# HGRN score matmuls in two stretches per head, the diagonal by products on GpSimd

## The chip, the cores and the metric

One core of one Trainium2 chip runs the whole program in one launch. The metric is the device time in microseconds (us) of one execution, and the comparison is the median over several executions. Engines are called PE (matrix engine), DVE (vector engine), ACT (scalar engine), POOL (GpSimd) and SP (the engine that issues most DMAs).

## What is computed

The reference is one inference step of a layer with two parallel branches, an mLSTM and an HGRN2, merged by sigmoid gates. A prompt of 512 frames and a running stream of 32 frames go through together (544 columns). The change touches only the HGRN2 branch: 8 heads of width 128, in which every head computes, in chunks of 64 frames,

```python
g = cumsum(lf)                                  # per channel, lf = log of the forget gate
dec = exp(where(causal, g[t] - g[s], -inf))
a = einsum('tc,tsc,sc->ts', q, dec, k)          # scores, decay per channel
o = einsum('tc,ce->te', q * exp(g), S) + einsum('ts,se->te', a, v)
S_new = exp(g_last)[:, None] * S + einsum('sc,se->ce', k * exp(g_last - g), v)
```

and then a head-wise RMS norm of `o`, times a gate. All is float32.

## The kernel before

**Layout.** Activations lie with channels on the 128 partitions and frames along the free dimension. The kernel treats the 512 prompt frames of a head as chunks of 128 (`chunks`), the first half in reversed order, with the 32 sample frames between the halves (`HB` = 288 is the border, `NA` = 256, `NS` = 32).

**Dense work.** PE runs the projections, those of the HGRN branch and the merge gates among them, as dense matmuls with 272 moving columns (`Two.run`, L609). Each weight is split into a high and a low part on ACT (L133) and DVE (L134), and some weight sums are formed by DMA: SP loads a tile (L495), POOL starts a second transfer that adds into it (L496), and a third one may follow (L582). POOL's DMA starts sit in the same in-order queue as its other instructions.

**The pump.** PE's order in this part is written by hand. `Pump.run` takes a generator and, for each number it yields, advances the dense stream by so many steps; one step is six dense matmuls. The generator is `chain(h)`, one per HGRN head; its matmuls are placed between the dense ones where it resumes. The instructions of the other engines are ordered by the scheduler, by priority; `tc.high_priority()` lifts what stands under it. A chain takes 28 steps (27 for head 0), as many as the dense work of one head, so that one chain follows the other.

**A chain.** The causal decay is applied level by level (`LEVELS` = 1, 2, 4, 8, 16, 32, 64). At level c, blocks of c keys meet the next block of c queries; then keys and queries are multiplied in place by the decay over c frames, on DVE (L1911, two halves, with the decay products `tn` built at L1914 and L1917). For each level PE multiplies a packed copy of the keys (`km`, ACT, L1879) with the queries, for four groups of 32 keys side by side (L1841), plus four matmuls for the sample frames on levels under 32 (L1844). Because the products are made in place, levels 2, 8 and 32 also take a packed copy of the queries (`oldq`, L1873) and of the sample's pair (`olds`, L1878), so that two levels can be multiplied in one stretch of PE. This gives four stretches of score matmuls in a head: the diagonal with level 1, levels 2 and 4, 8 and 16, 32 and 64.

The diagonal (q times k of the same frame, summed over channels) is made by 20 matmuls of 32 keys against 32 queries (L1894), of which DVE keeps the diagonal by a product with a mask (`eye`, L1921) and a reduction (L1922) into `dg`. ACT scales the transposed values by it into `ov` and `osb` (L1946, L1947), and DVE adds that to the output later (L1996, L1997).

`collect` brings scores from PSUM into the tile `at` (L1854 on DVE under a level mask, L1856 and L1860 on ACT). POOL spreads `near` and `far` into place (L1935) and cuts the triangles into `aa` (L1790). The rest of the chain: transposes of the values (`columns`, L1818, right after level 1), of the keys, the state update `su` (L1966, DVE L1972), and the output `ho` (L1990 to L1994). Then ACT squares the output (L2001, L2002), DVE computes the inverse root and scales (L2006, L2012). `finish(h - 1)` transposes the output of the head before and multiplies by its gate. PSUM for all of these comes from `paux`, a ring of two buffers.

## Time and profile before

| | |
|---|---|
| median of 3 runs | 1091.46 us (1091.30 to 1091.87) |
| the profiled execution | 1093.22 us in all, span 1091.5 us |
| granted PE clock | 1.00 |
| PE busy | 1082.2 us (99%) |
| DVE busy | 896.1 us (82%) |
| ACT busy | 700.6 us (64%) |
| POOL busy | 220.1 us (20%) |
| DMA | 176.67 MB, mean 162 GB/s |

A row of a group of instructions names line, engine, operation, output and inputs with their shapes, then the count; behind the bar stand the busy time in us and the mean ns of one, and behind the next bar the idle time just ahead of them with what ended most of it. A row of the timeline starts with the start in us from the beginning of the span and the duration; a count at its end means that several like it were merged. A row by stretch gives the window, its length, and then the busy us of PE, its weight loads, DVE, ACT and POOL. A row of waits gives who waited for whom, the total, how often, and the longest. A float32 matmul appears as two records; the dense matmuls with rounded operands (L609) as one.

### The profile page before, as it was taken

The numbers are of one execution on the slowest core, as the hardware profiler recorded it, in microseconds if no ns is written. First come the engines' busy times: TensorE is split into PE (matmuls) and PEld (weight loads), VectorE is DVE, ScalarE is ACT, GpSimd is POOL, SyncE is SP. The second block draws the span as 40 slices with busy tenths as digits, with TensorE's granted clock in tenths as the row PEclk, the third lists the DMA queues.
The fourth block names the chain that finished last, engine by engine and source line by source line (L and its number), as shares of the span: only waits on it lengthen the run. The fifth ranks groups of instructions, "written<-read, shape, count | busy, mean of one in ns | idle before, by whom it ended". The sixth has DMA issues, their size and how long they took to land.

```text
span 1091.5 us, 26220 instructions
## 1 busy us (share of the span) xinstructions
PE 1082.2 (99%) x9865; PEld 1055.3 (97%) x9865; DVE 896.1 (82%) x2052; ACT 700.6 (64%) x1611; POOL 220.1 (20%) x399
## 2 busy tenths in 40 slices
PE   9999999999999999999999999999999999999998
PEld 9899999999999999999999999999999999999997
DVE  7889988686897785986888688989999877778886
ACT  7767556754666564765557378877777666446673
POOL 5204010303021122202120032323333210000002
PEclk9999999999999999999999999999999999999999
DMA  7134515549454377545699666666666683337753
GB/s 237 54 124 145 173 59 175 152 135 211 131 170 154 122 171 168 176 164 176 187 245 256 184 158 138 150 152 157 152 146 160 172 225 98 112 91 243 232 199 121
DMA packets 97270, 176.67 MB, mean 162 GB/s; under 512 B 11412, under 2 KB 18580, under 8 KB 96888
## 3 DMA queue, kind: packets, MB, share of 16 engines
q1 hardware_dynamic: 81072, 140.96, 40.5%
q0 software_dynamic: 15184, 32.93, 16.6%
q8 instruction: 77, 1.26, 0.5%
q10 hardware_dynamic: 888, 1.12, 0.3%
q14 instruction: 49, 0.40, 0.1%
HBM read 150.05 MB, written 41.69 MB: 176 GB/s over the span
## 4 chain that ended last, share of the span: by engine, by line
PE 89%; DVE 4%; DMA 4%; issue 1%; ACT 1%; POOL 0%; ACTq 0%; DVEq 0%; SPq 0%; POOLq 0%
PE d L609 41%; PE ya L168 9%; PE yb L168 4%; PE q L168 4%; PE k L168 4%; PE C L1078 4%; PE sc L1038 2%; PE u L292 2%; PE d L461 2%; PE vp L1570 2%; PE nm L1258 2%; DMA ws<-in_w_in 2%; PE ple L168 1%; PE pl L1841 1%; DMA kv_d<-vhl 1%
## 5 line engine op out<-in xcount | busy, mean ns | idle before, releaser
L496 POOL DMA_DIRECT2D ws<-in_w_in x46 | 40.2, 875 | 198.0 <-DVE hkq L1911 61.2
L623 ACT COPY t<-d 128x272 f32<-128x272 f32 x153 | 57.9, 378 | 15.6 <-PE d L609 14.6
L1911 DVE TENSOR_TENSOR hkq<-hkq,q 128x288 f32<-128x288 f32 (+1 forms) x96 | 40.6, 429 | 4.0 <-PE pl L1844 3.4
L786 DVE SCALAR_TENSOR_TENSOR cv<-ub,vec,cv 128x547 f32<-128x547 f32 x48 | 37.6, 783 | 1.7 <-ACT cv L781 1.2
L1192 DVE SCALAR_TENSOR_TENSOR c<-c,wi,Cs 128x258 f32<-128x258 f32 x32 | 15.3, 479 | 18.8 <-PE Cs L1190 18.5
L1355 DVE TENSOR_TENSOR y<-ya,y 128x272 f32<-128x272 f32 x48 | 18.8, 434 | 14.3 <-PE ya L168 12.5
L1090 ACT COPY Co<-C 128x258 f32<-128x258 f32 x30 | 9.8, 378 | 27.2 <-PE C L1078 24.9
L778 POOL COPY uo<-ub 128x3 f32<-128x3 f32 x16 | 18.7, 1166 | 34.6 <-DVE ub L632 26.7
L134 POOL TENSOR_TENSOR wple50l<-wple5r,wple50h 128x256 fp32r<-128x256 f32 x1 | 0.7, 736 | 121.1 <-ACT wple50h L133 121.1
L962 POOL COPY ksm<-kf 128x96 f32<-128x96 f32 x16 | 7.1, 445 | 85.8 <-ACT kf L976 85.7
L1269 ACT COPY y<-nm 128x516 f32<-128x516 f32 x16 | 9.4, 590 | 22.9 <-PE nm L1258 22.5
L1879 ACT COPY km<-hkq 128x256 f32<-128x256 f32 x56 | 23.7, 424 | 0.0
L1935 POOL COPY at<-at 32x128 f32<-32x128 f32 x32 | 21.7, 678 | 8.4 <-DVE wa1282l L134 6.7
L962 POOL COPY vsm<-vt 128x96 f32<-128x96 f32 x12 | 5.7, 478 | 86.4 <-ACT vt L634 44.1
L582 POOL DMA_DIRECT2D ws<-in_w_in x14 | 12.8, 915 | 38.6 <-DVE ws272l L134 27.6
L1246 DVE BATCH_NORM_STATS2 bs<-y 128x6 f32<-128x512 f32 (+1 forms) x20 | 13.8, 691 | 8.2 <-ACT y L1269 7.8
L1258 PE MATMUL nm<-vhl,sh 128*128 128x258 f32 x112 | 18.4, 286 | 0.0
L2001 ACT ACTIVATE osq<-kq 128x128 f32<-128x128 f32 x32 | 9.8, 305 | 13.4 <-DVE kq L1996 13.1
L377 POOL DMA_DIRECT2D w_pg_d<-in_w_pg x16 | 13.1, 818 | 24.4 <-issue 20.2
L377 POOL DMA_DIRECT2D w_out_d<-in_w_out x16 | 13.5, 1004 | 14.3 <-issue 12.5
L1790 POOL TENSOR_SCALAR_AFFINE_SELECT aa<-at 128x128 f32<-128x128 f32 x32 | 16.1, 536 | 0.6
L1258 PEld LDWEIGHTS nm<-vhl,sh 128*128 128x128 f32 x112 | 15.4, 190 | 0.5 <-ACT Co L1090 0.3
(4739 smaller groups left out, 5095.3 us busy)
## 6 DMA issues: line engine op xcount, KB each, us to landing
ws<-in_w_in POOLq DMA_DIRECT2D x60, 256.0 KB, 5.1
ws<-in_w_in SPq DMA_DIRECT2D x46, 256.0 KB, 4.3
ya_d<-y SPq DMA_DIRECT2D x32, 272.0 KB, 2.3
y<-ya_d SPq DMA_DIRECT2D x24, 272.0 KB, 3.6
w_out_d<-in_w_out POOLq DMA_DIRECT2D x24, 256.0 KB, 6.6
w_pg_d<-in_w_pg POOLq DMA_DIRECT2D x24, 256.0 KB, 6.5
c<-in_C SPq DMA_DIRECT2D x16, 258.0 KB, 3.7
out_Cs<-c SPq DMA_DIRECT2D x16, 258.0 KB, 4.0
```

The costliest lines, as they stand in the source:

```text
L168: PE.matmul(both[b][:m, :TH], part(w, off + k * step, m, x), xx[:, half(b)], start=(k == 0 and j == 0), stop=(k == n - 1 and j == 2),)
L292: PE.matmul(both[b][:m, :TH], part(w, off + k * step, m, x), xx[:, half(b)], start=(k == 0 and j == 0), stop=(k == KD - 1 and j == 2),)
L377: G.dma_start(late[g][n][k], src, accum_op=ALU.add)
L461: PE.matmul(self.ps[b][:, : c.stop - c.start], part(self.w, k * P, P, x), xx[:, c], start=(k == 0 and j == 0), stop=(k == KD - 1 and j == 2),)
L496: G.dma_start(t, piece(u, i), accum_op=ALU.add)
L609: PE.matmul(ps, ww[:, c], xx, start=(start and k == 0 and j == 0), stop=end, skip_group_check=not start,)
L623: self.kept = S.copy(t, ps)
L786: V.scalar_tensor_tensor(cv[:, :547], ub[:, j : j + 547], vcol(V_CW + 4 * ft + j), cv[:, :547], ALU.mult, ALU.add)
L1078: PE.matmul(pn[g][:, :VH], kw[b][x][:, f * P : (f + 1) * P], vv[b][y][:, g * VH : (g + 1) * VH], start=(b == 0 and j == 0), stop=(b == NB ...
L1258: PE.matmul(pn[:, g, :VH], st[j][x][:, (i - j) * P : (i - j + 1) * P], vv[j][y][:, g * VH : (g + 1) * VH], start=(j == 0 and q == 0), stop ...
L1879: low = S.copy(km.rearrange("p (n j c) -> p n j c", j=2, c=c), view(kk, HB, ((2 * c, NA // (2 * c)), (c - HB, 2), (1, c))),)
L1911: V.tensor_tensor(x, x, d, ALU.mult)
```

## The change

The scores of a head are computed in two stretches instead of four: the diagonal with levels 1, 2, 4 and 8, and then levels 16, 32 and 64. For that, levels 1, 2, 4, 16 and 32 take packed copies of the queries (and levels 1, 2, 4 and 16 of the sample's pair), in tiles whose buffers other phases used (`more`, `asked`, `far_`, and the tile `q0`); level 64 reads its keys in place without a copy. The decay products `tn` move from `q0` into `tf`.

The diagonal: POOL multiplies queries and keys element by element (`q0 * kk`), and 20 matmuls against a matrix of two columns of ones sum over the channels. DVE copies the result to `dg`. POOL multiplies the identity by it into `ov` and adds that into the triangles `aa` (and, for the sample, into `near`), so the output matmul includes the diagonal. The scalings on ACT and the additions on DVE go; the squares and the scaling read the output from PSUM.

The steps between the parts of the chain change (`STEPS`, `TAILS`; 28 in all again), and levels 1 and 2 lose their high priority (`URGENT`).

```diff
-STEPS = (2, 3, 3, 3, 3, 3, 3)
+STEPS = (2, 2, 2, 4, 2, 2, 3)
+BEHIND, URGENT, TAILS = (1, 3, 5, 6), 2, (3, 2, 4)
+FIRSTS, LASTS = (0, 4), (3, 6)
...
             V.tensor_tensor(qq[:, :T], q0[:, :T], tf[:, :T], ALU.mult)
+            G.tensor_tensor(q0[:, :T], q0[:, :T], kk[:, :T], ALU.mult)
...
         for li, c in enumerate(LEVELS):
-            first_ = li % 2 == 1
-            if li % 2 == 1 or li == 0:
+            if li in FIRSTS:
                 kms = tp.tile([P, 2, NA], F32, tag="vs", name=f"km{h}{c}", bufs=1)
-            km = kms[:, 0 if li % 2 else 1]
+                if li == 0:
+                    more, asked = (tp.tile([P, NA + 4 * NS], F32, tag=g, ...) ... (("kx", "ksm"), ("qx", "vsm")))
+                    far_ = tp.tile([P, 2, NA], F32, tag="kws", name=f"kqx{h}", bufs=1)
+                    keeps = [(kms[:, 0], old), (kms[:, 1], asked[:, :NA]), (more[:, :NA], far_[:, 0]), (far_[:, 1], None)]
+                    rest = [more[:, NA : NA + 2 * NS], more[:, NA + 2 * NS :], asked[:, NA : NA + 2 * NS]]
+                else:
+                    keeps = [(kms[:, 0], q0[:, :NA]), (kms[:, 1], q0[:, NA : 2 * NA]), (None, None)]
+                    rest = [more[:, NA : NA + 2 * NS]]
+                held_ = []
+            n, last = len(held_), li in LASTS
+            km, oldq = keeps[n]
...
-            with tc.high_priority():
-                if first_:
+            with tc.high_priority() if li >= URGENT else nullcontext():
+                if not last:
                     S.copy(oldq..., view(qq, ...))
                     if c < NS:
                         S.copy(olds, hs[h]["pair"][:, :, csmp])
-                low = S.copy(km..., view(kk, ...))
-            if not first_:
+                if km is not None:
+                    low = S.copy(km..., view(kk, ...))
+            if li in BEHIND:
                 held.append(low)
-                yield STEPS[li] + (STEPS[li - 1] if li else 0)
-                pn = paux(f"pl{h}{c}")
-                if li:
-                    scores(pn, 0, c // 2, kms[:, 0], True)
-                else:
-                    ...  PE.matmul(pn[...], kk[:, t_], q0[:, t_], start=True, stop=True)
-                scores(pn, 1, c, km, False)
+            yield STEPS[li]
+            if last:
+                pn, at_ = paux(f"pl{h}{c}")[:, 0], 0
+                if li == LASTS[0]:
+                    ...  PE.matmul(pn[..., 2 * b : 2 * b + 2], q0[:, t_ : t_ + NS], ones, start=True, stop=True)
+                    at_ = 4 * NS
+                outs_ = []
+                for li_, c_, km_, oldq_, olds_ in held_:
+                    w = 3 * NS if c_ < NS else 2 * c_
+                    outs_.append((pn[:, at_ : at_ + w], li_, c_))
+                    scores(outs_[-1][0], c_, km_, oldq_, olds_)
+                    at_ += w
...
-            if not first_:
-                if li == 0:
-                    same = small("same", [P, NB + 1, NS], bufs=1, tag="vsm")
-                    V.tensor_tensor(same, pn[...], eye, ALU.mult)
-                    V.tensor_reduce(dg, same, AX.X, ALU.add)
-                else:
-                    collect(pn[:, 0], li - 1, c // 2)
-                collect(pn[:, 1], li, c)
+            if last:
+                for x in outs_:
+                    collect(*x)
+                if li == LASTS[0]:
+                    V.tensor_copy(dg, pn[:, : 2 * (NB + 1) : 2])
+                    G.tensor_tensor(ov[:, :NP]..., ident..., dg[:, :NB]..., ALU.mult)
+                    G.tensor_scalar(ov[:, NP:T], ident[:, :NS], dg[:, NB : NB + 1], None, ALU.mult)
+                    G.tensor_tensor(near[:, 2 * NS :], near[:, 2 * NS :], ov[:, NP:T], ALU.add)
...
                 columns(ii, it, its)
                 nc.sync.dma_start(s0, a["S0"][h])
-                for b in range(NB):
-                    S.mul(ov[:, b * P : (b + 1) * P], it[:, b * P : (b + 1) * P], dg[:, b : b + 1])
-                S.mul(osb, its, dg[:, 4:5])
...
                 triangle(aa[:, j, b], at[:, b * P : (b + 1) * P], 1 - 2 * j)
+            d = ov[:, 2 * j * P : 2 * (j + 1) * P].rearrange("p (b t) -> p b t", b=2)
+            G.tensor_tensor(aa[:, j], aa[:, j], d, ALU.add)
-        yield 2
+        yield TAILS[0]
         columns(kk, kt, kts)
-        yield 2
+        yield TAILS[1]
         pu = paux(f"su{h}")
...
-        yield 2
+        yield TAILS[2]
         po = paux(f"ho{h}")
...
-        with tc.high_priority():
-            V.tensor_tensor(ov[:, :NP], po[:, 0, :], ov[:, :NP], ALU.add)
-            V.tensor_tensor(osb, po[:, 1, :P], osb, ALU.add)
...
-            S.activation(osq, ov[:, b * P : (b + 1) * P], AF.Square, accum_out=hv[:, b : b + 1])
+            S.activation(osq, po[:, 0, b * P : (b + 1) * P], AF.Square, accum_out=hv[:, b : b + 1])
...
-            ov[:, :NP].rearrange("p (b e) -> p b e", b=NB),
+            po[:, 0].rearrange("p (b e) -> p b e", b=NB),
...
-        V.tensor_scalar(osb, osb, hr[:, NB : NB + 1], None, ALU.mult)
+        V.tensor_scalar(osb, po[:, 1, :P], hr[:, NB : NB + 1], None, ALU.mult)
```

More of the change, by code (lines that the diff above doesn't have):

```diff
@@ L1802, in chain @@
         qoff = qq.offset - kk.offset
-        ttmp, base = q0, 0
         tsmp = None
@@ L1822, in columns, with scores @@
                 S.copy(dss[:NS], pt[:NS, 1, :P])
-        def scores(pn, i, c, km, snap):
+        def scores(out, c, km, oldq, olds):
             for b in range(2):
@@ L1834, in scores @@
                             ask = view(qq, b * P + 2 * n * c + (0 if j else HB + c), ((1, c),))
-                    elif snap:
+                    elif oldq is not None:
                         ask = oldq[:, key : key + NS]
-                    elif c > 1:
+                    else:
                         ask = view(qq, key, ((2 * c, NS // (2 * c)), (HB + c, 2), (1, c)))
-                    else:
-                        out, ask = out.rearrange("p (i s) -> p s i", s=2), view(qq, key, ((HB + 1, 2), (2, NS // 2)))
-                    PE.matmul(out, km[:, key : key + NS], ask, start=True, stop=True)
+                    if km is not None:
+                        keys = km[:, key : key + NS]
+                    else:
+                        keys = view(kk, b * P + g * NS % c + 2 * n * c + (c if j else HB), ((1, NS),))
+                    PE.matmul(d, keys, ask, start=True, stop=True)
             if c < NS:
@@ L1892, in chain @@
+            if li in BEHIND:
+                held.append(low)
+            yield STEPS[li]
+            if last:
+                pn, at_ = paux(f"pl{h}{c}")[:, 0], 0
+                if li == LASTS[0]:
+                    for b, (c_, _, _) in enumerate((chunks[1], chunks[0], *chunks[2:], (csmp, 0, 0))):
                         for g in range(QUADS):
-                            t_ = slice(c_.start + (g * NS if b < NB else 0), c_.start + (g * NS if b < NB else 0) + NS)
+                            t_ = c_.start + (g * NS if b < NB else 0)
@@ L1898, in chain @@
             nb, na = (HB if c < NS else NA) // (2 * c), NA // (2 * c)
             tb, ta = told[:, : 2 * nb], told[:, told.shape[-1] - 2 * na :]
-            tn = ttmp[:, base : base + nb + na]
+            tn = tf[:, : nb + na]
             sides = ((tb, 0, nb, 1, 0), (ta, HB, na, 0, nb))
-            with tc.high_priority():
+            with tc.high_priority() if li >= URGENT else nullcontext():
                 for t, lo, m, first, _ in sides:
@@ L1967, in chain @@
         PE.matmul(pu[:, 1, :P], kts, its, start=True, stop=True)
-        sb = tf
+        sb = q0
         with tc.high_priority():
@@ L1994, in chain @@
         PE.matmul(po[:, 1, :P], qq[:, NA : NA + P], s0, start=False, stop=True)
[L1995 to L1997 removed]
         hv, hr = small("hv", [P, 5]), small("hr", [P, 5])
[L1999 removed]
+        osq = its
         for b in range(NB):
[L2001 to L2002 removed]
+            S.activation(osq, po[:, 0, b * P : (b + 1) * P], AF.Square, accum_out=hv[:, b : b + 1])
+        S.activation(osq, po[:, 1, :P], AF.Square, accum_out=hv[:, NB : NB + 1])
         with tc.high_priority() if h == HH - 2 else nullcontext():
```

45 lines of the change are left out of this document (24 added, 21 removed).

## The prediction

> **What bounds the kernel now.** I read the page first (busy shares, the chain that ended last), then the busy times of the HGRN stretch, then what the matrix engine (PE) waited for there.
>
> ```profile
> PE 1082.2 (99%) x9865; PEld 1055.3 (97%) x9865; DVE 896.1 (82%) x2052; ACT 700.6 (64%) x1611; POOL 220.1 (20%) x399
> PE 89%; DVE 4%; DMA 4%; issue 1%; ACT 1%; POOL 0%; ACTq 0%; DVEq 0%; SPq 0%; POOLq 0%
> ...
> 625.00:865.00 240.00, 238.00 (x3259) 230.25 (x3259) 216.53 (x616) 185.08 (x526) 80.52 (x123) 1.00 0.66 154
> ...
> PE ht L1818 <- DVE hkq L1911: 1.4, 2, 0.8
> ```
>
> PE is busy 99% of the span and carries 89% of the chain that ended last. In the 240 us that hold the eight heads PE is busy 238.0, DVE 216.5, ACT 185.1, POOL 80.5, at a granted clock of 1.00. So only PE time saved or PE waits moved can change the end; the other three matter through waits. The stretch is a stream of dense matmuls into which a head's chain puts short bursts. Busy time hides what a burst costs, since small matmuls overlap; I take the cost from the starts around it. This is head 5 (PE in order of time):
>
> ```profile
> 793.20 0.29 PE L609 MATMUL d<-xfh,ws378h 128*128 128x272 f32 x1
> ...
> 793.45 0.29 PE L609 MATMUL d<-xfh,ws378l 128*128 128x272 f32 x1
> 793.67 0.33 PE L1841 MATMUL pl<-lmask,km 128*32 128x32 f32 x16
> 793.82 0.41 PE L1841 MATMUL pl<-hkq,km 128*32 128x64 f32 x16
> 794.15 0.39 PE L609 MATMUL d<-xh,wa1155h 128*128 128x272 f32 x1
> 794.38 0.29 PE L609 MATMUL d<-xl,wa1155h 128*128 128x272 f32 x1
> ...
> 781.59 0.28 PE L609 MATMUL d<-xh,wa1178l 128*128 128x272 f32 x1
> 781.80 0.33 PE L1841 MATMUL pl<-lmask,km 128*32 128x32 f32 x16
> 781.95 0.25 PE L1844 MATMUL pl<-lmask 128*32 128x32 f32 x8
> ...
> 782.17 0.26 PE L1844 MATMUL pl<-hkq 128*32 128x32 f32 x7
> 782.36 0.40 PE L609 MATMUL d<-xh,wa1178h 128*128 128x272 f32 x1
> 782.59 0.30 PE L609 MATMUL d<-xl,wa1178h 128*128 128x272 f32 x1
> ...
> 774.86 0.28 PE L609 MATMUL d<-xh,ws477l 128*128 128x272 f32 x1
> 775.07 0.53 PE L1894 MATMUL pl<-q,hkq 128*32 128x32 f32 x38
> ...
> 775.59 0.26 PE L1844 MATMUL pl<-hkq 128*32 128x32 f32 x7
> 775.78 0.40 PE L609 MATMUL d<-xfh,ws254h 128*128 128x272 f32 x1
> 776.01 0.29 PE L609 MATMUL d<-xfl,ws254h 128*128 128x272 f32 x1
> ...
> L1894 PE MATMUL pl<-q,hkq x320: 196/196/217, 628.1 to 833.7; 128*32 128x32 f32 x160
> ```
>
> Dense matmuls start 0.126 us apart (793.20 to 793.45 is two of them); a pump step is six, 0.76 us. Each fp32 matmul leaves two records: the diagonal is 320/8 = 40 a head, a level under 32 is 16 + 8 = 24 (781.80, 781.95), levels 32 and 64 are 16 each. Cost of a burst = start of the second dense matmul behind it, minus the last one before it, minus 0.25:
> - levels 2 and 4, 48 records: 782.59 - 781.59 - 0.25 = 0.75 us
> - diagonal and level 1, 64 records: 776.01 - 774.86 - 0.25 = 0.90
> - levels 32 and 64, 16 + 16 records: 794.38 - 793.45 - 0.25 = 0.68
>
> From the first two, a 32-column record costs 0.15/16 = 9.4 ns and a burst has a fixed price of 0.75 - 48 x 0.0094 = 0.30 us: the late first record (0.21 after the last dense start) and the slow restart (0.23 between the first two dense starts). From the third, a 64-column record costs (0.68 - 0.30 - 0.15)/16 = 14.4 ns.
>
> **The change, part by part.** *Two bursts for four.* Today a head pays 0.90 + 0.75 + 0.75 (levels 8 and 16, again 48 records) + 0.68 = 3.08. The first new burst has 40 + 4 x 24 = 136 records: 0.30 + 1.28 = 1.58. The second has levels 16 (24), 32 (16) and 64 (16 wide): 0.30 + 0.38 + 0.23 = 0.91. Saved: 0.59 us a head, two fixed prices; over eight heads **-4.8 us**.
>
> *Two-column diagonal.* The 40 diagonal records keep 32 columns of weights but stream 2 columns instead of 32. From 9.4 and 14.4 ns a column costs 0.16 ns, so at best a record falls to 4.7 ns: -0.19 a head, -1.5 in all. If load and issue set the price, 0. A loss is excluded, since nothing streams longer. I take the middle, **-0.8**, as neither row has so few columns.
> The Trainium skill (TensorE: Matmul & The Clock Gate, Back-to-back issue gap) gives one price for all widths from 1 to 64 columns; this trace disagrees, 9.4 against 14.4 ns, and by the rule this term would be 0 and the sum -4.2.
>
> *The stall in front of the key transposes.* In head 1 four records of the key transpose are split:
>
> ```profile
> 677.70 0.38 PE L1818 MATMUL ht<-ident,hkq 128*128 128x128 f32 x2
> 678.93 0.44 PE L1818 MATMUL ht<-ident,hkq 128*128 128x128 f32 x2 [0.85 <-DVE hkq L1911]
> ```
>
> PE waits for DVE's level-64 product; two heads have it, 1.4 us of PE idle together (the row of waits above). The transposes come 3 steps behind the scores instead of 2 (TAILS), 0.76 us of air for each: up to 1.4 gone, at worst 0, if what holds DVE up holds up the next step's operands instead. I take **-1.0**.
>
> *ACT and DVE work, all beside PE.*
>
> ```profile
> L1879 ACT COPY km<-hkq 128x256 f32<-128x256 f32 x55 | 23.2, 422 | 0.0
> L1946 ACT ACTIVATE kq<-hi,dg 128x128 f32<-128x128 f32 x32 | 11.1, 392 | 0.0
> L1873 ACT COPY lmask<-hkq 128x256 f32<-128x256 f32 x24 | 10.2, 427 | 8.2 <-DVE hkq L1911 8.2
> ...
> L1996 DVE TENSOR_TENSOR kq<-ho,kq 128x512 f32<-128x512 f32 x8 | 5.5, 691 | 2.2 <-PE ho L1994 2.2
> ...
> 787.90 0.46 DVE L1911 TENSOR_TENSOR hkq<-hkq,q 128x288 f32<-128x288 f32 x1 [0.55 <-PE pl L1844]
> ...
> 792.24 0.40 ACT L1879 COPY km<-hkq 128x256 f32<-128x256 f32 x1
> ```
>
> ACT loses four diagonal scalings (4 x 0.39) and one key copy (0.42), gains two query copies (0.85): about -1.1 a head. DVE loses the 0.69 add, the mask product and small companions, and gains a five-column copy. Both get lighter, so no throughput bound appears: 0.
>
> *Latency in front of the bursts.* A level needs its copies on ACT and then its products on DVE. Today the stretch from level 16's products (787.90) to level 64's key copy (done 792.64) holds two levels: 4.7 us, 2.4 a level, with everything that DVE and ACT do between. Afterwards the first burst comes 2 + 1 + 2 + 2 + 4 = 11 steps (8.3 us) and the value transposes (0.5, an estimate: with the state update they fill the 1.8 us that six steps leave of the 6.35 under GpSimd) behind the chain's start, for three levels and one copy: 7.1 + 0.4 = 7.5. The second comes 2 + 1 + 2 + 3 = 8 steps (6.1 us) and the output transposes of the head before (0.5 again) behind the first, for levels 8, 16 and 32: 7.1 at the old pace, 4.5 if nothing stood between (3 x 0.85 of products, 1.1 and 0.85 of copies). So the first has 0.8 of air, the second lacks 0.5 at worst and has 2.1 at best. Bounds: 0 and 0.5 x 8 = 4.0; I take 0.1 a head, **+0.8**, nearer the lower end, since a mask product, its reduction and two additions have left DVE.
>
> *GpSimd.* Nearest rows:
>
> ```profile
> L1023 POOL TENSOR_TENSOR qw<-qf,wi 128x32 f32<-128x32 f32 x16 | 6.2, 414 | 22.7 <-ACT qf L1003 22.6
> L2205 POOL TENSOR_TENSOR h<-h,rows 128x272 f32<-128x272 f32 x6 | 4.5, 776 | 55.3 <-ACT rows L2201 55.3
> ...
> 794.98 0.87 POOL L496 DMA_DIRECT2D ws<-in_w_in  x1 [4.74 <-DVE hkq L1911]
> 795.60 3.44 POOL L1935 COPY at<-at 32x128 f32<-32x128 f32 x4
> 799.11 1.83 POOL L1790 TENSOR_SCALAR_AFFINE_SELECT aa<-at 128x128 f32<-128x128 f32 x4
> ...
> 800.50 0.71 PE L1990 MATMUL ho<-hi,aa 128*128 128x128 f32 x4
> ```
>
> From 414 ns at 32 columns and 776 at 272, 1.5 ns a column: 1.19 (queries times keys, 544) + 1.14 (diagonals, 512) + 2 x 0.41 (sample) + 2 x 0.75 (adds into the triangles) = 4.7 us a head, on an engine busy 10 of 30. What counts is the tail: today from the end of the level-64 burst (794.15) the copies start after 1.45, take 3.51, the triangles 1.83, and PE asks for them at 800.50, 6.35 us on: POOL is the tighter side already. Afterwards it needs 1.45 + 3.51 + 1.83 + 1.50 = 8.3, and PE's three more steps ask at 6.35 + 2.27 = 8.6. It fits by 0.3, and the first output matmul needs only half. Bounds: 0 a head, or 1.2 (slow rival). I take 0.1 a head, **+0.8**, as the margin is near none.
>
> Sum: -4.8 - 0.8 - 1.0 + 0.8 + 0.8 = **-5.0 us**. The profiled span is 1091.5 (its run 1093.22 in all); the median of the runs is 1091.46, so the span serves as base: **1086.5 us**.
>
> **Rivals.** *GpSimd's queue (slower).* The weight-sum transfers (L496) sit in the same in-order queue; the one at 794.98 held it for 4.74 us, just ahead of the copies. The second burst is now three steps further from the output matmuls, but if that transfer stays ahead and keeps its place in PE's stream, the copies start 2.3 us later behind the burst: first half ready at 3.7 + 3.5 + 0.9 + 0.75 = 8.9 against 8.6, second at 10.6 against 9.5 with the wait added for the first, 1.1 to 1.2 us a head. In eight heads +9.6 in place of +0.8: 1095.3. It turns slower than before from 0.7 us a head. Against it: a list order may put the copies first.
>
> *The output bank is held (same).* Today a DVE add empties the output PSUM early; afterwards the bank stays until the scaled copy.
>
> ```profile
> 773.26 0.39 PE L1994 MATMUL ho<-s,hkq 128*128 128x128 f32 x2
> ...
> 784.49 0.28 DVE L2012 TENSOR_SCALAR osb<-osb,hr 128x128 f32<-128x128 f32 x1
> ```
>
> The scaling ends at 784.8, 11.1 us behind the output matmuls (773.7). With two buffers the second request after them needs that bank: today the transposes, afterwards the first burst, 8.3 + 0.5 = 8.8 us on. The squares start 1.0 earlier without the adds, which gives 10.1; levels 1 and 2 lose their priority over this work, which may give the rest (the four products of 0.85 in pairs are 1.7). If nothing does, 1.3 us in each of 7 heads, 9.1, and 1095.6; if half of it stays, 4.2 and 1090.7, which is the case I weigh here.
>
> *The fixed price is no price of a burst (same).* If the long burst waits on its own operands or costs more per record, the 4.8 go: 1091.3.
>
> *Shared ports (same).*
>
> ```profile
> 799.52 0.78 DVE L134 TENSOR_TENSOR ws355l<-ws,ws355h 128x512 fp32r<-128x512 f32 x1
> ...
> 801.24 0.69 DVE L134 TENSOR_TENSOR wa1179l<-wi79r,wa1179h 128x512 fp32r<-128x512 f32 x1 [0.30 <-PE ho L1990]
> ```
>
> Beside POOL's triangles the split takes 0.78, else 0.69: 13%. On 4.7 us of new POOL work that is 0.6 us of DVE a head, under the 1.0 removed; if it all fell on the bursts, 4.8: 1091.3. The Trainium skill (GPSIMD Engine Reference, Key points) says that the two engines contend when DVE has two SBUF inputs; this row agrees.
>
> **How the numbers follow.** Forecast 0.58; held bank 0.18 (a fifth of it in its full, slower form); fixed price 0.05; ports 0.04; queue 0.15. A 0.2% change is 2.2 us, about what a measurement here can tell. Faster 0.58 (the forecast), same 0.23 (mild bank, fixed price, ports), slower 0.19 (queue, full bank). The likeliest's own range: with the good ends -4.8 - 1.5 - 1.4 = 1083.8, with no gain but the bursts and 0.15 a head in each of the two waits -4.8 + 2.4 = 1089.1. For 8 in 10 I go from 1083.0 to 1094.5, which leaves out the worst of the queue and of the bank.
>
> **What would show it.** Right: two stretches of score matmuls a head, costing about 1.4 to 1.6 and 0.9 us by the starts around them; no long PE wait; the diagonal records closer than 9 ns. Wrong: PE waiting on POOL at the output matmuls, or on ACT or DVE at a score stretch (the scaled output copy for the first, level products for the second); weight-sum transfers that land later with splits waited for.

## The result, and the profile after

The change made the kernel slower: 1104.59 us median (1103.30 to 1106.77) against 1091.38 for the kernel before on the same chip, a ratio of 1.0119 with a 95% interval of 1.0106 to 1.0132. Forecast were 1086.5 us, and 1094.5 as the upper end. The profiled execution took 1105.38 us, its span is 1103.7. Line numbers below are those of the changed kernel (an experiment's can be a few higher): dense matmuls L611, score matmuls L1842 and L1845, diagonal L1906, level products L1929, GpSimd's product of queries and keys L1720.

The page: busy time by engine, and the chain that ended last by engine.

```profile
PE 1082.3 (98%) x9865; PEld 1055.4 (96%) x9865; DVE 909.7 (82%) x2027; ACT 699.1 (63%) x1595; POOL 260.0 (24%) x447
...
PE 84%; DVE 6%; ACT 3%; DMA 3%; issue 2%; POOL 1%; SPq 0%; DVEq 0%; ACTq 0%; POOLq 0%
```

PE is as busy as before (1082.2), so the 12 us of span are idle time of PE; its share of the chain fell from 89 to 84%. POOL has 40 us more, DVE 14 us more although it was given less to do. The stretch that holds the heads, in the view of busy times by stretch:

```profile
625.00:865.00 240.00, 226.29 (x3165) 219.33 (x3164) 220.05 (x569) 173.88 (x480) 114.44 (x163) 0.99 0.64 149
```

PE is busy 226.3 of the 240 us; it was 238.0. What PE waited for (total, times, longest):

```profile
PE ht L1817 <- DVE hkq L1929: 6.0, 4, 2.3
PE su L1987 <- ACT hkq L1820: 3.8, 5, 2.3
PE pl L1842 <- DVE hkq L1929: 2.0, 1, 2.0
PE ho L2011 <- POOL aa L1977: 1.4, 4, 0.5
```

Before, the one wait in this list from the heads was 1.4 us at the key transposes (`ht`). Now a head waits there, at the state update (`su`) and at the output (`ho`): all three stand behind the second stretch. The 2.0 us at `pl` are a single wait, in front of the second stretch of the last head.

The two stretches themselves cost what was forecast. Head 4, PE in order of time:

```profile
757.54 0.29 PE L611 MATMUL d<-xh,wa1277l 128*128 128x272 f32 x1
757.76 0.50 PE L1906 MATMUL pl<-ones,q 128*32 128x2 f32 x39
758.10 0.17 PE L1906 MATMUL pl<-ones,q 128*32 128x2 f32 x1
...
759.27 0.29 PE L611 MATMUL d<-xl,wa1277h 128*128 128x272 f32 x1
...
765.57 0.29 PE L611 MATMUL d<-xfh,ws177l 128*128 128x272 f32 x1
...
766.74 0.29 PE L611 MATMUL d<-xfl,ws177h 128*128 128x272 f32 x1
```

By the starts around them, as in the prediction: 759.27 - 757.54 - 0.25 = 1.48 us (forecast 1.58 with the diagonal at the old price, 1.48 with the 0.8 us of the two columns) and 766.74 - 765.57 - 0.25 = 0.92 (forecast 0.91). The same reading over all bursts gives a table of what each cost above its undisturbed price (before 0.90, 0.75, 0.75, 0.68 for the stretches, after 1.48 and 0.92; `ht` 0.55, `su` 1.12, `ho` 2.01, output transposes 0.55), summed over the eight heads in us, "dense" being gaps between dense matmuls:

| kernel | stretches | ht | su | ho | rest and dense | sum |
|---|---|---|---|---|---|---|
| before | 0.3 | 2.1 | 0.1 | 0.5 | 0.7 | 3.7 |
| the change | 2.9 | 6.9 | 6.3 | 2.5 | 1.7 | 20.3 |
| e1 product on DVE | 4.2 | 4.1 | 0.3 | 5.7 | 0.1 | 14.4 |
| e8 = e1, steps 5, 2, 2 behind | 2.4 | 0.0 | 0.0 | 11.9 | 1.5 | 15.9 |
| e7 = e1, short tail | 3.9 | 3.8 | 0.0 | 0.1 | 3.2 | 10.9 |
| e12 = e7, product on POOL | 5.3 | 10.2 | 8.2 | 0.0 | 2.8 | 26.6 |
| e9 = the change, steps moved | 12.9 | 0.2 | 2.5 | 4.9 | 11.4 | 31.9 |

The undisturbed price of the stretches fell from 24.6 to 19.2 us, 5.4 saved, and the waits rose by 16.6: together +11.2 of the 12.2 us of span.

Where the waits at `ht` and `su` come from, same head, all engines in order of time:

```profile
767.65 0.42 DVE L1929 TENSOR_TENSOR hkq<-hkq,tf 128x256 f32<-128x256 f32 x1
...
768.59 2.27 DVE L1929 TENSOR_TENSOR hkq<-hkq,tf 128x256 f32<-128x256 f32 x1
...
768.89 0.38 PE L1817 MATMUL ht<-ident,hkq 128*128 128x128 f32 x2
768.96 1.61 POOL L1720 TENSOR_TENSOR q<-q,hkq 128x544 f32<-128x544 f32 x1
...
770.92 0.44 PE L1817 MATMUL ht<-ident,hkq 128*128 128x128 f32 x2 [1.65 <-DVE hkq L1929]
...
771.14 0.21 ACT L1857 COPY at<-pl 128x64 f32<-128x64 f32 x1 [2.02 <-DVE at L1855]
```

The level-64 product has two halves on DVE. The first takes 0.42 us, the second, of the same shape, 2.27: POOL's product of the next head's queries and keys lies beside it, and DVE comes free 0.29 us after that ends (768.96 + 1.61 = 770.57; 770.86). PE waits 1.65 us for it, and ACT, behind DVE's collection of the scores, is 2.02 us late, so its copy of the transposed keys comes late for `su`. DVE records of 1.6 to 2.5 us stand beside L1720 in all seven heads in which it ran within these 240 us. Which record it meets decides what that costs. In three heads it is the level-64 product, and in one a weight split ahead of that product: there the excess at `ht` is 1.2 to 2.6 us. In one head it is a 128x4 decay product ahead of the collection (2.16 us in place of 0.15), and the excess comes at `su`, 2.5 us. In the other two it is a weight split that the chain does not need next, and hardly anything is lost.

What places the product is also POOL's in-order list. Its operand, DVE's query product (L1719), was done at 767.14, yet it started at 768.96, right behind a weight-sum transfer that had waited for ACT:

```profile
768.30 0.90 POOL L498 DMA_DIRECT2D ws<-in_w_in  x1 [2.88 <-ACT kx L1891]
```

Such a transfer stands right ahead of L1720 in six of the seven heads. What the product would have met without it was not tried. POOL's own work, by line and shape in the stretch of the heads:

```profile
L1958 POOL COPY at<-at 32x128 f32<-32x128 f32 x32 | 16.7, 520 | 7.1 <-ACT at L1857 6.1
L1792 POOL TENSOR_SCALAR_AFFINE_SELECT aa<-at 128x128 f32<-128x128 f32 x32 | 15.6, 509 | 0.6
L1977 POOL TENSOR_TENSOR aa<-aa,kq 128x256 f32<-128x256 f32 x16 | 15.5, 971 | 0.7
L1720 POOL TENSOR_TENSOR q<-q,hkq 128x544 f32<-128x544 f32 x7 | 11.7, 1670 | 1.3 <-DVE hkq L1719 1.3
```

### The profile page after: what moved, and what is told of

Read it like the earlier page. It is cut to its first block, busy times and chain, and to the rows that moved or that the text cites. A ratio compares the mean times of both kernels' runs of the same rounds, so it can differ in the third digit from the quotient of the medians.

```text
span 1103.7 us, 26253 instructions
## 1 busy us (share of the span) xinstructions
PE 1082.3 (98%) x9865; PEld 1055.4 (96%) x9865; DVE 909.7 (82%) x2027; ACT 699.1 (63%) x1595; POOL 260.0 (24%) x447
## 3 DMA queue, kind: packets, MB, share of 16 engines
q10 hardware_dynamic: 888, 1.12, 0.3%
## 4 chain that ended last, share of the span: by engine, by line
PE 84%; DVE 6%; ACT 3%; DMA 3%; issue 2%; POOL 1%; SPq 0%; DVEq 0%; ACTq 0%; POOLq 0%
PE d L611 38%; PE ya L170 9%; PE yb L170 4%; PE q L170 4%; PE k L170 4%; PE C L1080 4%; PE nm L1260 3%; PE sc L1040 2%; PE u L294 2%; PE d L463 2%; PE vp L1571 2%; DVE hkq L1929 1%; PE ple L170 1%; PE su L1987 1%; DMA ws<-in_w_in 1%
## 5 line engine op out<-in xcount | busy, mean ns | idle before, releaser
L498 POOL DMA_DIRECT2D ws<-in_w_in x46 | 40.6, 882 | 165.8 <-DMA ws<-in_w_in 29.5
L1929 DVE TENSOR_TENSOR hkq<-hkq,tf 128x288 f32<-128x288 f32 (+1 forms) x112 | 57.9, 518 | 4.7 <-ACT kx L1893 1.2
L780 POOL COPY uo<-ub 128x3 f32<-128x3 f32 x16 | 18.7, 1167 | 34.5 <-DVE ub L634 26.6
L1260 PE MATMUL nm<-vhl,sh 128*128 128x258 f32 x112 | 18.4, 286 | 0.0
L1958 POOL COPY at<-at 32x128 f32<-32x128 f32 x32 | 16.7, 520 | 7.1 <-ACT at L1857 6.1
L584 POOL DMA_DIRECT2D ws<-in_w_in x14 | 15.5, 1110 | 10.9 <-DVE y L1357 10.7
L2223 POOL TENSOR_TENSOR h<-h,rows 128x272 f32<-128x272 f32 x6 | 4.5, 775 | 55.4 <-ACT rows L2219 55.4
L1720 POOL TENSOR_TENSOR q<-q,hkq 128x544 f32<-128x544 f32 x8 | 13.0, 1631 | 17.9 <-ACT wa1172h L135 16.6
L781 POOL COPY uo<-ub 128x3 f32<-128x3 f32 x16 | 4.4, 274 | 51.1 <-DVE ub L632 38.8
L1009 DVE TENSOR_TENSOR ql<-q,qh 128x272 fp32r<-128x272 f32 x24 | 9.4, 434 | 8.3 <-ACT qh L1008 7.2
```

What stands on the lines that cost most here:

```text
L498: G.dma_start(t, piece(u, i), accum_op=ALU.add)
L1260: PE.matmul(pn[:, g, :VH], st[j][x][:, (i - j) * P : (i - j + 1) * P], vv[j][y][:, g * VH : (g + 1) * VH], start=(j == 0 and q == 0), stop ...
L1929: V.tensor_tensor(x, x, d, ALU.mult)
```

## The experiments

Theories: A, GpSimd's products stop DVE's two-input products beside them. B, the two stretches with their steps leave too little air in themselves. C, GpSimd's tail behind the second stretch is late. Formed later: M, the air stands in the wrong place; D, VectorE has lost throughput, which comes back wherever the steps are cut. Ratios are to the kernel before, with their 95% intervals.

### Which part of the change: e1 to e4

e1, one instruction moved; the order of the matmuls stays:

```diff
-            G.tensor_tensor(q0[:, :T], q0[:, :T], kk[:, :T], ALU.mult)
+            V.tensor_tensor(q0[:, :T], q0[:, :T], kk[:, :T], ALU.mult)
```

> The changed kernel with one instruction a head moved: the product of queries and keys (128x544) is made by VectorE instead of GpSimd; the order of the matmuls is the same. Theory A (a two-input product of GpSimd holds up VectorE's two-input products beside it, the level-64 product comes late, and TensorE waits for the key transposes and then for the state update): the waits of ht for hkq (6.0 us) and of su (3.8 us) mostly go, VectorE pays 8 x 0.75 us more beside TensorE, and the time is 1092 to 1096. Theory B (two long stretches with their step counts leave too little air, whoever makes the products): VectorE is even busier, so 1102 to 1107. Theory C (GpSimd's queue and tail: the triangles come late): only 1.67 us of 5.7 a head leave GpSimd, well ahead of the tail, so 1101 to 1105.

1100.81 us, 1.0081 (1.0062 to 1.0100): 4 us less than the change, just under what C gave and far from A's. The waits turn round:

```profile
PE ho L2011 <- POOL aa L1977: 3.7, 7, 0.6
PE ht L1817 <- DVE hkq L1929: 2.6, 5, 0.5
```

The wait at `su` is gone and the one at `ht` less than halved, but the wait for POOL at `ho`, 1.4 before, is now 3.7: what PE had lost earlier had given POOL its time.

e2, the change without any two-input operation of the diagonal on POOL:

```diff
+            V.tensor_tensor(q0[:, :T], q0[:, :T], kk[:, :T], ALU.mult)
...
+                    S.mul(ov[:, b * P : (b + 1) * P], it[:, b * P : (b + 1) * P], dg[:, b : b + 1])
...
+            V.tensor_tensor(ov[:, :NP], po[:, 0, :], ov[:, :NP], ALU.add)
```

> The changed kernel with no two-input operation of the diagonal left on GpSimd: the product is VectorE's, ScalarE scales the values by the diagonal, VectorE adds them to the output (0.69 us a head) as in the kernel before; the two stretches and the two-column matmuls stay. Theory A: the forecast's -4.8 and -0.8 come true and the waits fall to those of before: 1085 to 1089. Theory B: 1101 to 1106. Theory C: as theory A, 1085 to 1090, so this run alone does not part A from C; e1 does.

1103.70 us, 1.0105 (1.0090 to 1.0120); the diagonals of the first two blocks are exchanged in it, which alters values and no amount of work. Every theory but B missed. Of 18.4 us of excess, 10.1 are at `ho`, nearly all in two heads where the triangles came 5 us late: POOL's copies started 6.7 and 6.5 us behind the stretch there, after 4.1 and 3.1 us of waiting for ACT's collection (L1857). Removing the products from POOL is not enough.

e3, the two stretches with the old diagonal (in a third, short one ahead of them); the edit takes the prediction's lines for `dg`, `ov` and the adds back.

> The changed kernel's two stretches and query copies alone: the diagonal is made and applied as before (32-column matmuls, mask and sum on VectorE, values scaled by ScalarE) and has a short stretch of its own, three stretches a head in all. By the prices of the prediction 0.30 + 0.38 for it, 0.30 + 0.90 and 0.91: 2.79 against 3.08 a head, -2.3 in all. Theory A and C: 1088 to 1092. Theory B: the waits stay, 1100 to 1105.

1105.64 us, 1.0132 (1.0109 to 1.0156): where B put it, or just above. Nearly all of it, 15.1 us of 16.8, stands in one place, the first stretch:

```profile
PE pl L1842 <- ACT kqx L1905: 13.9, 8, 1.9
```

With the old path ACT squares the sum that DVE has added, and scales the values by the diagonal, before its query copies for level 2; the first stretch is 2.0 us late by starts in seven heads. In the change the squares read PSUM and the scalings are gone.

e4, the four stretches of before with the new diagonal and the new output path.

> The kernel before, with its four stretches, and the new diagonal alone: GpSimd products, two-column matmuls, adds into the triangles. Theory A: the collisions come without the stretches: 1097 to 1106. Theory B: 1088 to 1092 (the -0.8 of the two columns, waits as before). Theory C: the triangles get two more adds (2 x 0.97 us) with only two steps in front of the output instead of four: 1099 to 1107, with the wait at the output matmuls (ho for aa) instead of at the key transposes (ht for hkq).

1152.09 us, 1.0551 (1.0534 to 1.0567), beyond every theory:

```profile
PE ht L1819 <- DVE hr L186: 31.2, 6, 5.2
```

The row names DVE's inverse root of the output of the head before (L186). In time, all engines of one such head, it is another thing that ends the wait:

```profile
667.27 0.25 POOL L1929 TENSOR_TENSOR at<-at,kq 128x32 f32<-128x32 f32 x1
667.56 0.26 DVE L1855 COPY_PREDICATED at<-lmask,pl 128x96 f32<-128x96 uint8 x1 [0.64 <-POOL at L1929]
...
667.97 1.09 PE L1819 MATMUL ht<-ident,hi 128*128 128x128 f32 x4 [5.19 <-DVE hr L186]
...
669.12 0.69 DVE L2009 TENSOR_TENSOR kq<-ho,hr 128x512 f32<-128x512 f32 x1
```

The value transposes start 0.15 us after DVE's collection of the first stretch's scores (L1855) ends, and so they do in seven of the eight heads; they start 1.15 us before DVE first reads the output for its scaling (L2009). The kernel uses two such PSUM buffers in turn. The output of the head before still holds one, since it is now read from PSUM, and the other was the first stretch's until its scores were collected: this is how I read the order, no run parts the two. DVE collected late because it waited for POOL's add of the sample's diagonal (L1929), behind POOL's diagonal product (1.63 us here). So this is near the prediction's rival of the held bank but not its form: the bank is held, and PE waits for the other one. It hides what the products cost here, so e4 doesn't part A from C.

### What a GpSimd operation costs: e5, e6, e12, e16

e5 puts a product that nobody reads back on POOL in e1; e6 a copy of the same shape.

```diff
+            idle = small("idle", [P, T // 2], dt=mybir.dt.bfloat16, bufs=1)
+            for b_ in range(2):
+                s_ = slice(b_ * T // 2, (b_ + 1) * T // 2)
+                G.tensor_tensor(idle, q0[:, s_], kk[:, s_], ALU.mult)      # e6: G.tensor_copy(idle, q0[:, s_])
```

> The kernel of e1 (product by VectorE) with a product that nobody reads put back on GpSimd in the old place, in two halves of 128x272, in scratch: same order of matmuls, same VectorE work. e1 took 4 us off the change. Theory A (two-input operations of GpSimd stop VectorE's two-input operations for their whole length): VectorE records of 1 to 2 us come back right behind the second stretch, the waits of ht for hkq return, 1103 to 1107. Rival (e1 gained because GpSimd's queue got shorter, not because of the ports): the same 1103 to 1107 here, but then e6 shows it too. Rival (e1's gain was chance in the order of VectorE's work): 1099 to 1102.

> As e5, but the unused work on GpSimd is a copy with one input, in the same two halves and place, so GpSimd is held nearly as long. Theory A: no long VectorE record, 1100 to 1102, the time of e1. Rival (queue of GpSimd, or any traffic of it): 1103 to 1106.

e5 1110.79 us, 1.0169 (1.0151 to 1.0187); e6 1105.65, 1.0122 (1.0107 to 1.0137). e5 lies beyond every range put on it, e6 where the rival against A put it: the copy alone costs 4.8 us over e1, the product 5.1 us more. At `ht` all three kernels have an excess of 4.0 to 4.1, and the excess at `ho` is 16.7 in e5, 12.6 in e6 and 5.7 in e1. In e5 that is POOL's queue: its quarter copies (L1962) start directly behind the idle product, of 2.0 to 3.0 us, in all seven heads. In e6 they do so in two heads only, and in the others wait 0.2 to 0.5 us for ACT; 5.0 of the 6.9 us that it has more at `ho` than e1 are in the first head, where the copies stand directly behind 3.2 us of idle copies. The rest of e6's loss is spread thin over the heads and not told apart. The product of e5 read DVE's result and so started behind the level-64 product, not beside it; its place was a bad one for the test. What the copy does to DVE can be read off e6, all engines in order of time:

```profile
742.77 2.06 POOL L1724 CAST idle<-q 128x272 bf16<-128x272 f32 x2
...
743.01 0.73 DVE L136 TENSOR_TENSOR wa2276l<-wi68r,wa2276h 128x512 fp32r<-128x512 f32 x1
743.66 0.89 DVE L136 TENSOR_TENSOR ws476l<-ws,ws476h 128x512 fp32r<-128x512 f32 x1
```

Two-input splits beside it take 0.73 and 0.89 in place of 0.69, not the length of the copy.

e12 is e7 (next group: product on DVE, short tail) with L1720 back on POOL.

> e7 with the product of queries and keys back on GpSimd, so against e7 only this instruction differs, and against the change only the tail. Theory A (the product stops VectorE's level-64 product in most heads): long VectorE records of 1.6 to 2.5 us beside it, waits at ht and su, 1099 to 1103. If the product cost the change only through GpSimd's queue and tail, the short tail absorbs it: 1094 to 1097.

1112.80 us, 1.0194 (1.0177 to 1.0211), against 1.0034 for e7: 16.9 us for the engine of one instruction a head, more than A asked. The waits, and one collision:

```profile
PE ht L1819 <- DVE hkq L1931: 8.0, 6, 2.2
PE su L1990 <- ACT hkq L1822: 6.4, 6, 2.4
```

```profile
773.54 2.10 DVE L1931 TENSOR_TENSOR hkq<-hkq,tf 128x256 f32<-128x256 f32 x1
773.72 1.62 POOL L1722 TENSOR_TENSOR q<-q,hkq 128x544 f32<-128x544 f32 x1
```

With the long tail the same move (the change against e1) was worth only 3.8, since POOL's lateness stood behind it.

e16 cuts POOL's product in the change into four of 128x136.

> The changed kernel with GpSimd's product of queries and keys cut into four of 128x136, one after the other; nothing else differs. In e5, where an unused product ran in two halves, VectorE's records beside it grew by some 0.4 to 0.6 us each, not by the whole product, and went on at normal length between. If the two engines exclude each other instruction by instruction: no VectorE record beside the product over about 1.2 us, the excess at ht and su (13.2 us by starts) halves, 1098 to 1102. If they share a bandwidth, or VectorE waits until GpSimd's queue is empty: records of 1.6 to 2.5 us stay, 1103 to 1107.

1107.13 us, 1.0131 (1.0113 to 1.0149): no help. The excess is 3.8 us at `ht`, 7.5 at `su` and now 9.1 at `ho`.

```profile
771.89 2.40 DVE L1931 TENSOR_TENSOR hkq<-hkq,tf 128x256 f32<-128x256 f32 x1
771.98 2.02 POOL L1722 TENSOR_TENSOR q<-q,hkq 128x136 f32<-128x136 f32 x4
```

Here DVE's product waits for all four. That is so in four of the seven heads (DVE records of 2.3 to 2.4 us); in the other three the engines take turns, with DVE records of 0.7 to 1.0 us between POOL's pieces. Cutting the product lets DVE in between sometimes, not always, and it made nothing faster.

### The tail and the steps: e7 to e11, e13 to e15, e17

e7 shortens POOL's tail in e1: the diagonals go straight into `aa` in the middle of the head, and DVE lays the strict triangles over them under a mask.

```diff
+                    G.tensor_tensor(aa.rearrange("p j b t -> p (j b) t"), ident..., dg[:, :NB]..., ALU.mult)
...
-                triangle(aa[:, j, b], at[:, b * P : (b + 1) * P], 1 - 2 * j)
-            G.tensor_tensor(aa[:, j], aa[:, j], d, ALU.add)
+            V.copy_predicated(aa[:, j], tri[:, j]..., at[:, :NA].rearrange("p (b t) -> p b t", b=2))
```

> The kernel of e1 with GpSimd's tail shortened: the diagonals are laid into the triangle tile in the middle of the head (the 128x512 product writes there), and at the end VectorE lays the strict triangles over them with two predicated copies of 128x256 in place of four GpSimd triangles and two GpSimd adds (3.7 us a head). Theory C for what is left of the loss (the tail of GpSimd sets when the output matmuls start, 0.85 us a head in e1): the waits of ho for aa (3.7 us in the records, 5.6 by starts) go and 1093 to 1097 comes out. Theory B (VectorE's queue has no room: its copies now wait for GpSimd's quarter copies and hold its splits): 1099 to 1104, with PE waiting at ht, su or d.

1095.92 us, 1.0034 (1.0021 to 1.0048): as C said; no wait at `ho` is left. It is the best of the altered kernels, still above the kernel before.

e8 is e1 with `TAILS` 5, 2, 2 in place of 3, 2, 4.

> The kernel of e1 with the same nine steps behind the second stretch cut otherwise: 5, 2, 2 in place of 3, 2, 4, so the key transposes come 1.5 us later and the output matmuls where they were. If the level-64 product alone is late (theory A and B), the 3.3 us of excess at ht go: 1096 to 1098. If GpSimd's tail stands behind it (theory C), the 0.85 us of air that the wait at ht gave is missing at ho and comes back there: 1099 to 1102.

1099.33 us, 1.0064 (1.0049 to 1.0079): as C said, at its edge. The 4 us at `ht` go and come back at `ho`:

```profile
PE ho L2011 <- POOL aa L1977: 8.2, 13, 1.1
```

By starts 11.9 us, 1.3 to 1.9 in each of seven heads: how late POOL's tail really is. It starts late, in that head 3.6 us behind the stretch:

```profile
763.82 0.41 PE L1842 MATMUL pl<-hkq 128*32 128x64 f32 x14
...
767.25 0.26 DVE L1855 COPY_PREDICATED at<-lmask,pl 128x96 f32<-128x96 uint8 x1
...
767.82 2.52 POOL L1958 COPY at<-at 32x128 f32<-32x128 f32 x4 [0.74 <-ACT at L1857]
```

e9, e10 and e11 take three steps from in front of the first stretch and put them behind it, in the change, in e1 and in e7.

```diff
-STEPS = (2, 2, 2, 4, 2, 2, 3); TAILS = (3, 2, 4)
+STEPS = (2, 2, 2, 1, 2, 2, 3); TAILS = (6, 2, 4)      # e9; e10 and e11: (2, 2, 2, 1, 2, 2, 4) and (5, 2, 4)
```

> The changed kernel with step counts alone altered, the sum per head kept: three steps (2.3 us of dense matmuls) taken from in front of the first stretch and put between the second stretch and the key transposes: STEPS 2,2,2,1,2,2,3 and TAILS 6,2,4. In the trace of the change the last operand of the first stretch (ScalarE's copy kqx) is done 5.7 to 7.3 us ahead of it, while behind the second stretch the transposes are 0.7 to 2.5 us late and GpSimd's triangles 1.7 to 1.9 (e8). Theory M (the work is not too much, the margin stands in the wrong place; collisions and GpSimd's tail cost only because no air stands behind the second stretch): the excess at ht, su and ho (15.7 us by starts) nearly goes, 1088 to 1093. Theory D (VectorE's lost time is a loss of throughput that comes back somewhere else): 1098 to 1104.

> e1 (product on VectorE) with three steps moved: STEPS 2,2,2,1,2,2,4 and TAILS 5,2,4, so one step more in front of the second stretch and two in front of the transposes. Theory M: the 3.3 us at ht and 5.6 at ho go as far as 1.5 us of air reach (GpSimd's tail was 1.7 to 1.9 late with none): 1091 to 1094. Theory D: 1098 to 1101.

> e7 (product and triangles on VectorE) with the steps of e10: STEPS 2,2,2,1,2,2,4 and TAILS 5,2,4. In e7 the triangles were done 2 us before the output matmuls, so only the 3.6 us of excess at the key transposes and 1.8 at the second stretches are left to take. Theory M: 1089 to 1092, level with or under the kernel before. Theory D: 1094 to 1097.

1117.38 us (1.0234, 1.0219 to 1.0249), 1107.71 (1.0146, 1.0131 to 1.0162) and 1115.03 (1.0211, 1.0195 to 1.0226): each slower than its base and above the ranges of M and of D alike. Theory M fell, and D's forecast missed too. The waits behind the second stretch did go (table, e9), but others came: those at `pl` in e9 stand in front of the second stretches, 10.7 of the 12.9 us by starts. e9, then e11:

```profile
PE pl L1842 <- DVE hkq L1929: 7.1, 8, 2.5
PE d L611 <- ACT t L625: 7.0, 11, 1.5
```

```profile
PE hoT L2041 <- DVE osb L2033: 11.0, 5, 2.7
```

The seven microseconds in front of the first stretch are not idle: ACT and DVE square, root and scale the output of the head before in them. Moved forward, the stretch drags the output transposes (three steps behind it) ahead of that scaling, or ACT's copies of dense results (`t`) come behind it.

e13 is e7 with `TAILS` 5, 2, 2.

> e7 (product and triangles on VectorE, two stretches) with the nine steps behind the second stretch cut 5, 2, 2 in place of 3, 2, 4, the cut that took the wait at the key transposes away in e8; nothing ahead of the first stretch is touched. In e7 the triangles were done 2 us before the output matmuls. If e9 to e11 failed because the first stretch was moved: the 3.6 us of excess at ht go, 1091 to 1093.5. If any other cut upsets the order of VectorE's and ScalarE's work: 1095 to 1101.

1100.29 us, 1.0077 (1.0063 to 1.0091): `ht` is free, but two steps are then too few from `su` to `ho`, 10.5 us by starts.

```profile
742.38 0.62 ACT L135 CAST ws253h<-ws 128x512 fp32r<-128x512 f32 x1 [3.07 <-DVE ws L572]
...
743.43 0.26 ACT L1994 COPY q<-su 128x128 f32<-128x128 f32 x1
```

The 0.26 us copy of the state stands behind two weight splits in ACT's in-order list, and the first of these waits 3.07 us for a weight sum of DVE. The kernel before has the same two splits ahead of that copy, and the same two steps; there the first split waits 1.11 us in the same head and PE not at all.

e14 drops the product: the diagonal comes from 32-column matmuls inside the first stretch, with a mask and a sum on DVE. It is made there from keys that levels 1 to 4 have already decayed, so its values are others, its work the same. e15 is e14 with `TAILS` 4, 2, 3.

```diff
-                                pn[..., 2 * b : 2 * b + 2], q0[:, t_ : t_ + NS], ones, start=True, stop=True
+                                both_banks[..., 1, b * NS : (b + 1) * NS], kk[:, t_ : t_ + NS], q0[:, t_ : t_ + NS], start=True, stop=True
...
-                    V.tensor_copy(dg, pn[:, : 2 * (NB + 1) : 2])
+                    V.tensor_tensor(same, both_banks[:, 1, ...], eye, ALU.mult)
+                    V.tensor_reduce(dg, same, AX.X, ALU.add)
```

> e7 without any product of queries and keys: the diagonal comes from 32-column matmuls of keys and queries inside the first stretch (40 records, by the rows 9.4 against 8.6 ns, so 0.3 us in all), and VectorE takes it out with a mask product and a sum (0.63 us a head) behind the first stretch in place of the 0.72 ahead of the level-64 product. Two stretches and predicated triangles stay. If the product in VectorE's list is what makes the level-64 product 0.85 us late in e1 and e7: 1092 to 1094. If not: 1095 to 1098.

> e14 with the steps behind the second stretch cut 4, 2, 3: one step more in front of the key transposes, the output matmuls where they were. If a rest of the wait at ht is left in e14, it goes: 1091 to 1093, level with the kernel before; else as e14.

1109.22 us (1.0162, 1.0148 to 1.0177) and 1107.24 (1.0141, 1.0127 to 1.0154): both missed, by the queue of POOL. e14:

```profile
739.33 0.88 POOL L498 DMA_DIRECT2D ws<-in_w_in  x1 [6.93 <-DVE hkq L1722]
...
741.74 0.25 POOL L1955 TENSOR_TENSOR at<-at,kq 128x32 f32<-128x32 f32 x1
742.03 0.27 DVE L1857 COPY_PREDICATED at<-lmask,pl 128x96 f32<-128x96 uint8 x1 [2.32 <-POOL at L1955]
```

A weight-sum transfer came to stand ahead of the diagonals in POOL's list and waited 6.93 us; DVE's collection waited for the sample's add, ACT for DVE, and PE at `su`. Whether the product was the cause of e7's late level-64 product is not told by these two.

e17 is e7 with DVE's product moved from behind the queries to the start of its own head's chain.

> e7, the best of the altered kernels so far, with VectorE's product of queries and keys (0.72 us) taken out of the place ahead of the level-64 product of the head before and put at the start of its own head's chain, ahead of the level-1 products; there the first stretch's last operand was done 5 us early. If that one record makes the level-64 product 0.85 us late: the 3.6 us of excess at the key transposes go and 1091.5 to 1093.5 comes out, level with the kernel before. If the order of the lists gives the time back in another place, as in e9 to e11 and e13: 1096 to 1103.

1096.86 us, 1.0048 (1.0034 to 1.0062): no gain.

```profile
PE ht L1819 <- DVE hkq L1931: 2.5, 6, 0.5
...
PE su L1990 <- ACT hkq L1822: 2.0, 6, 0.4
```

The waits at `ht` stay as they were, and 3.7 us by starts come at `su`, where e7 had none. This does not clear the product: in its old place, ahead of the second half of the level-64 product, a weight split of the same length now stands in DVE's list.

```profile
734.89 0.69 DVE L136 TENSOR_TENSOR wa1253l<-wi53r,wa1253h 128x512 fp32r<-128x512 f32 x1
```

The two halves lie at 734.55 and 735.49 around it. In e7 the product stood between them, for 0.72 us, and this split behind them. Whatever the list puts there makes the second half late; what the half would be without either was not run. What would have to be reordered to reach the kernel before stays open; no version here beats it.

## Why the prediction was wrong, step by step

- **Two bursts for four (-4.8) and two-column diagonal (-0.8).** Held in the sum: 5.4 us by the prices above against 5.6. Not in the reading of the columns: 39 two-column records start within 758.10 - 757.76 = 0.34 us, 8.7 ns each; the other 96 of the first stretch cost (1.48 - 0.30 - 0.34)/96 = 8.8 ns if the fixed price is 0.30. With the diagonal at 32 columns (e14) the first stretch takes 1.49 us in every head, against 1.47 in the change: 2 columns instead of 32 brought 0.02 us a head, and nearly all of the 5.4 is the bursts'. The Trainium skill's one price for 1 to 64 columns (TensorE: Matmul & The Clock Gate, Back-to-back issue gap), set aside in the prediction, agrees here between 2 and 32.
- **Stall in front of the key transposes (-1.0).** Wrong in sign: the excess at `ht` went from 2.1 to 6.9 us, and 6.3 at `su` came with it. The upper bound was 0, "if what holds DVE up holds up the next step's operands"; a new stall in the same place was not considered.
- **ACT and DVE lighter (0).** The step that failed. DVE was given 25 instructions fewer and was busy 13.6 us longer. The rival of shared ports had the mechanism right and its size wrong: 13% of POOL's time, read off POOL's triangles (one input) beside a split. Beside POOL's two-input product DVE's lasts until POOL is done: 2.27 us in place of 0.42. It was to stay "under the 1.0 removed" and got a chance of 0.04; measured it is 16.9 us where nothing else hides it (e12 against e7), 3.8 in the change (against e1). The busy sum on DVE could not show it, because the place makes the price: beside the one product that PE asks for next it is dear, beside a split behind it nearly free.
- **GpSimd (+0.8).** The second failing term: 8.3 us were to be needed and 8.6 to be there. In the head of e8 shown above it is 764.23 to 774.80, 10.6 us. Copies, triangles and adds together were close (2.5 + 2.2 + 2.1, forecast 3.5 + 1.8 + 1.5). The start was not: 3.6 us behind the stretch instead of 1.45, since DVE's collection stands in its list behind the next head's query products and two splits. In the change itself the copies of that head start 771.42 - 766.58 = 4.8 us behind the stretch. The price is 11.9 us in e8, 5.7 in e1, where the wait at `ht` covers part, and 2.5 in the change, where the waits at `ht` and `su` had given POOL its time.
- **Latency in front of the bursts (+0.8).** The distribution was wrong. The first stretch was to have 0.8 us of air (by the prediction's own terms 8.3 + 0.5 - 7.5 = 1.3, since the 0.5 of the value transposes was counted for the second stretch only; the sum does not use it). In this head its last operand is done 7 us ahead of the first stretch:

```profile
750.30 0.41 ACT L1893 COPY kqx<-hkq 128x256 f32<-128x256 f32 x1
```

  The copy ends at 750.71, the stretch starts at 757.76. That air is taken by the output of the head before (e9, e11), so it can't be spent. The second stretch, which was to lack 0.5, is late by more than 0.2 us in one head of the change only.
- **The rivals.** Held bank: no such wait in the change, and the premise, that the first stretch needs that buffer, falls with e7, where it starts before the output is scaled:

```profile
723.85 0.50 PE L1908 MATMUL pl<-ones,q 128*32 128x2 f32 x39
...
725.27 0.69 DVE L2027 TENSOR_TENSOR kq<-ho,hr 128x512 f32<-128x512 f32 x1
```

  In e4 the held bank is there, but what ends the wait is the collection out of the other one. GpSimd's queue: in the change the quarter copies stand right behind POOL's own product in two heads and wait for ACT's collection in the others, never for a transfer; but a transfer does hold back the product itself (L498, above), and with it where the product meets DVE. In e14 and e15 a transfer holds the tail too. Fixed price not per burst: refuted by the stretches.
- **Why the sum broke.** The terms were priced one by one and added. Behind the second stretch they stand in one line (level-64 product, transposes, ACT's copy, state update, three DVE steps, output), with POOL's tail beside it, and 9 steps for all of it. A wait in the line gives POOL time, a shorter tail uncovers the line: the same instruction is worth 3.8 or 16.9 us. What is left in e7, 4.5 us against the kernel before, is not explained by these runs.

## What to carry to other kernels

Before work is given to an engine that is idle most of the time, look at what its instructions will lie beside, not at how long they are: a two-input GpSimd product placed beside a VectorE product that PE is about to ask for costs about its length on the bound, 1.2 to 2.6 us of PE in each such head here. In a chain with a fixed number of steps, list for each part when its last operand is done and when PE asks, and include the collection that starts the other engine's tail; air in one place may belong to another head's work. When a wait is removed and the time hardly moves, look for the wait that it had been covering, by cutting the steps differently (e8) before cutting work.

## What the runs showed of the hardware

With two inputs on both sides, one of the two engines stood still until the other was done: 0.42 us became 1.9 to 2.4 beside a POOL product of 1.6 to 2.0, and a 128x4 product of 0.15 us became 2.16. By the recorded starts it is not always the later one that stands: in the two collisions shown above, of the change and of e12, DVE's record starts 0.37 and 0.18 us ahead of POOL's and is the one that is held. POOL's product is lengthened in its turn: 1.88 us beside a split that began 0.02 us earlier and kept its 0.69, 1.36 where no two-input DVE record lay beside it. Four short POOL products back to back held DVE for the whole run in four of seven heads (e16); in three the engines took turns. Two one-input copies, 2.06 us together, lengthened DVE's two-input splits only from 0.69 to 0.73 and 0.89 (e6). Where PE waited longest, in e4, the granted clock was 0.91 and 0.89 in the two halves of the heads' stretch, against 1.00 before. In the change it was 0.50 for some 2 us right behind a long wait of PE (862.4 to 864.3), with dense matmuls 0.23 us apart instead of 0.126. So part of a long wait's price comes behind it: by counting such starts, an estimate, some 1.3 us in the change and some 10 us in e4.

The Trainium skill (SBUF — State Buffer, SBUF: two separate sides) describes an exclusive lock on a shared pair of ports, kept for the whole instruction, with the other engine blocked. e12 agrees in the block; e16 agrees in three heads and goes beyond one instruction in four; the one-input copy of e6 did not block, so there the measurement differs from the Trainium skill, and it decides.
